# Shifting where float32r operands start in SBUF, by 64 and 128 bytes

## The chip, the cores and the metric

One core of one Trainium2 chip. The metric is the device time of one execution in microseconds: the median of the timed runs.

## What is computed

A block of two layers on a sequence of 512 tokens with 1024 channels, all in float32. Each layer has a mixer and a SwiGLU feed-forward network (FFN, inner width 2816), both between RMS norms with scales, shifts and gates that come from a condition vector:

```python
for layer in range(DEPTH):
    mod = (cond @ ada_w[layer] + ada_b[layer])[:, None, :]
    sh1, sc1, g1, sh2, sc2, g2 = jnp.split(mod, 6, axis=-1)
    u = rms_norm(h, norm_g[layer, 0]) * (1.0 + sc1) + sh1
    ...
    h = h + (1.0 + g1) * rms_norm(y, norm_g[layer, 1])
    u = rms_norm(h, norm_g[layer, 2]) * (1.0 + sc2) + sh2
    y = swiglu_ffn(u, ffn_w_in[layer], ffn_w_out[layer])
    h = h + (1.0 + g2) * rms_norm(y, norm_g[layer, 3])
```

The mixer of layer 0 is a gated recurrence (HGRN, chunks of 32 tokens, 8 heads of 128). That of layer 1 is attention in three dilated groups with 8 heads each; its input projection makes queries, keys and values for each group.

## The kernel before

**Products in three.** Weights and activations are float32. Each is cut into a float32r tile "hi" and a float32r rest "lo", and a product is three matmuls into one bank: hi by hi, hi by lo, lo by hi. `three` (lines 430 to 433) issues them, and nearly all matmuls of the kernel come from it. `block` (line 435) has weights as the stationary operand and activations as the moving one; products by token (lines 1190 and 1361, `prods` in `mixer_out` and `ffn`) have it the other way round, with 512 columns of weights moving.

**The weight stream.** `Stream` (line 36) loads 1 MB pieces of weights through SyncE's queue into two places "raw", then ScalarE copies hi and VectorE subtracts lo. hi and lo have three places each (tags "hi" and "lo" in the pool "weights"), 2048 float32r per partition. Pieces for the quarter products ("quarters", "half") are cut by the stage that uses them; it takes places of the same tags through `part_tiles` (line 119).

**Quarter products.** Part of the FFN's input product and two of the attention's value projections are done as a 2 x 2 block product with seven products in place of eight. `seven_products` (line 764) does one column block of gate and up per step. Stationary: quarters of the weights and of their sums, in the tiles hiq and loq (and, for one of two sets, the tiles "spare"). Moving: uh and ul, 256 columns at a time, or th and tl, which hold sums of quarters of the activations. Each step has seven runs of four times three matmuls, 84 in all; three runs read uh and ul, four read th and tl. There are 16 steps in layer 0's FFN and 18 in layer 1's. `seven_values` (line 1365) does the same for the values by token: here the quarters of the weights are the moving operand and uh and ul (as th and tl), apart and the like are stationary.

**Other products.** The HGRN projections, queries and keys, one value group, the mixers' output projections and the FFN's output product have 512 moving columns. After each mixer, in `mixer_out`, the first FFN blocks are done in halves of 256 columns (`half`, line 677, and lines 707 and 710). Scores, transposes and probabilities by values use plain float32.

**Where tiles lie.** Tile pools take SBUF from the left or the right side, each tile behind the last one of its pool. The pool "base" stands first on the left, with h, ident, ones, small columns, lb, omlb, uh and ul; "weights" follows with raw, hi and lo. apart lies on the right in the attention. A few tiles named "pad" only take room. In the built program before, every float32r operand of a matmul starts at 192 modulo 256 bytes in its partition, but for th and tl, which start at 128. Modulo 512 the numbers are the same.

**Order.** Most stages have their order written out by hand (`manual_schedule`); the others are ordered when the program is built.

Of the kernel before, what the change touches and what calls it, by code (L numbers as in the profile page):

```python
# [9 lines left out]
F32 = mybir.dt.float32  # L10
F32R = mybir.dt.float32r
# [4 lines left out]
P = 128  # L16
S = 512
D = 1024
KT = D // P
# [11 lines left out]
C3 = float(np.float32(TWO_PI - C1 - C2))  # L31
MAGIC = 12582912.0
WHOLE = ("quarters", "half")


class Stream:
# [41 lines left out]
    def process_to(self, end):  # L78
        while self.done < end:
            self.fill()  # L80
            i = self.done
            kind = self.items[i][0]
            t = self.raw.pop(i)
            if kind == "w":
                hi = self.pool.tile([P, 2048], F32R, name=f"hi{i}", tag="hi", bufs=self.parts)
                lo = self.pool.tile([P, 2048], F32R, name=f"lo{i}", tag="lo", bufs=self.parts)
                self.nc.scalar.copy(hi, t)  # L87
                self.nc.vector.tensor_sub(lo, t, hi.bitcast(F32))  # L88
                self.ready.append((hi, lo))
            else:  # L90
                self.items[i][2](t)
            self.done += 1
        self.fill()

    def pieces(self, n, flat=False):

        i = self.done
        t = self.raw.pop(i)
        hi = self.pool.tile([P, 2048], F32R, name=f"hi{i}", tag="hi", bufs=self.parts)
        lo = self.pool.tile([P, 2048], F32R, name=f"lo{i}", tag="lo", bufs=self.parts)  # L100
        self.ready.append((hi, lo))
        self.done += 1
        rows = 1 if flat else KT
        size = 2048 // rows // n
        cut = lambda a, k: a.rearrange("p (k c) -> p k c", k=rows)[:, :, k * size:(k + 1) * size]

        def pair(k):
            return (lambda: self.nc.scalar.copy(cut(hi, k), cut(t, k)),  # L108
                    lambda: self.nc.vector.tensor_sub(cut(lo, k), cut(t, k), cut(hi, k).bitcast(F32)))
        return [pair(k) for k in range(n)]  # L110

    def whole(self):

        assert self.items[self.done][0] in WHOLE
        self.fill()
        self.done += 1
        return self.raw.pop(self.done - 1)

    def part_tiles(self):

        self.count = getattr(self, "count", 0) + 1
        return [self.pool.tile([P, 2048], F32R, name=f"{tag}q{self.count}", tag=tag, bufs=self.parts) for tag in ("hi", "lo")]

    def take(self, ahead=None):
        ahead = self.parts - 1 if ahead is None else ahead
        k = min(self.taken + ahead, len(self.wpos) - 1)
        stop = next((i for i in range(self.done, len(self.items)) if self.items[i][0] in WHOLE), len(self.items))
        self.process_to(min(self.wpos[k] + 1, stop))
# [26 lines left out]
def block_kernel(tc, x, c, positions, ada_w, ada_b, norm_g, hgrn_w_in, lower, hgrn_norm_g, hgrn_w_out,  # L155
# [6 lines left out]
    R4 = lambda a: a.rearrange("p (r l) -> p l r", r=4)  # L162

    with ExitStack() as ctx:
        base = ctx.enter_context(tc.tile_pool(name="base", bufs=1))
        wp = ctx.enter_context(tc.tile_pool(name="weights", bufs=1))
        psum = ctx.enter_context(tc.tile_pool(name="psum", bufs=1, space=bass.MemoryType.PSUM))
# [7 lines left out]
        def fresh(p, shape, tag, bufs=1, dt=F32):  # L175
            uid[0] += 1
            return p.tile(shape, dt, name=f"{tag}{uid[0]}", tag=tag, bufs=bufs)


        tcx = ctx.enter_context(ExitStack())  # L180
        cond_tiles = tcx.enter_context(tc.tile_pool(name="tiled", bufs=1, side="right")).tile([P, KT, 32], F32, name="cond_tiles")
        pre = ctx.enter_context(ExitStack())
        sp = pre.enter_context(tc.tile_pool(name="start", bufs=1, side="right"))
        rowsC = sp.tile([8, P], F32, name="rowsC")
# [4 lines left out]

        ident = base.tile([P, P], F32, name="ident")  # L190
        make_identity(nc, ident)
        ones = base.tile([P, P], F32, name="ones")
        pool.memset(ones, 1.0)
        expo = base.tile([P, 4], F32, name="expo")
        pool.memset(expo, -0.5)
# [219 lines left out]
        st = Stream(nc, wp, items, 2, 3)  # L415
# [2 lines left out]

        lb = base.tile([P, 8], F32, name="lb")
        omlb = base.tile([P, 8], F32, name="omlb")
        uh = base.tile([P, KT, S], F32R, name="uh")
        ul = base.tile([P, KT, S], F32R, name="ul")

# [9 lines left out]
        def block(whi, wlo, c0, width, ps=None, tok=slice(0, S), kts=range(KT), u=(uh, ul)):  # L435

            ps = bank("mm") if ps is None else ps
            for kt in kts:
                a = kt * width + c0
                three(ps[:, tok], whi[:, a:a + P], wlo[:, a:a + P], u[0][:, kt, tok], u[1][:, kt, tok], kt == 0, kt == KT - 1)  # L440
            return ps
# [304 lines left out]
        def token_sums(th, tl, room, uh=uh, ul=ul):  # L746


            q = lambda a, k: a[:, k // 2 * 4:k // 2 * 4 + 4, k % 2 * 256:k % 2 * 256 + 256].bitcast(F32)
            t = [room[:, 2 * k:2 * k + 2].rearrange("p a (b n) -> p (a b) n", b=2) for k in range(4)]  # L750
            for k in (0, 1, 3, 2):
                dve.tensor_add(t[k], q(uh, k), q(ul, k))
            dve.tensor_sub(t[0], t[0], t[1])
            dve.tensor_sub(t[1], t[3], t[1])
            dve.scalar_tensor_tensor(t[3], t[0], -1.0, t[3], op0=OP.mult, op1=OP.subtract)
            dve.scalar_tensor_tensor(t[2], t[3], -1.0, t[2], op0=OP.mult, op1=OP.subtract)

            def cut():
                for k in (3, 0, 2, 1):
                    act.copy(th[:, k], t[k])  # L760
                    dve.tensor_sub(tl[:, k], t[k], th[:, k].bitcast(F32))
            return cut

        def seven_products(fs, mid, sgp, spare, th, tl):
# [12 lines left out]
            ring = []  # L777
            raw, g_of = {}, {}

            def places(i):  # L780

                p = i % 2
                if len(ring) <= p:
                    ring.append((spare if p == 0 else st.part_tiles(), st.part_tiles()))
                return ring[p]

            def r_hi(i):
                if i < len(fs):
                    raw[i] = st.whole()
                    act.copy(places(i)[0][0][:, 0:1536], raw[i][:, 512:])  # L790

            def r_lo(i):
                hi, lo = places(i)[0]
                dve.tensor_sub(lo[:, 0:1536], raw[i][:, 512:], hi[:, 0:1536].bitcast(F32))  # L794
# [13 lines left out]
            def s_cut(i, k):  # L808
                src = Q4(raw[i])[:, 1:3] if k == 0 else Q4(raw[i])[:, 0:4:3]
                return [Q4(t)[:, 2 * k:2 * k + 2] for t in places(i)[1]] + [src]  # L810
# [84 lines left out]
        def ffn(l, first, close, nxt, side):  # L895
            turns.close()
            close()
            with ExitStack() as fx:
# [4 lines left out]
                with ExitStack() as qx:  # L903
                    sgp = qx.enter_context(tc.tile_pool(name=f"sg{l}", bufs=1, side=side))
                    qp = qx.enter_context(tc.tile_pool(name=f"quarters{l}", bufs=1, side=bass.opposite_side(side)))
                    spare = [qp.tile([P, 3 * 512], F32R, name=f"spare{l}{k}") for k in range(2)]
                    qp.tile([P, 112], F32, name=f"pad_q{l}")
                    th = qp.tile([P, 4, 4, 256], F32R, name=f"th{l}")
                    tl = qp.tile([P, 4, 4, 256], F32R, name=f"tl{l}")
                    for j in range(PLAIN[l]):  # L910
                        if j == 0:
                            pss = first
                        else:
                            pss = []
                            for i in range(2):
                                w = st.take()
                                pss += [block(*w, k * P, 256) for k in range(2)]
                        sg = [fresh(sgp, [P, S], "sg", 2) for _ in range(2)]
                        for k in range(2):
                            act.activation(sg[k], pss[k], AF.Silu)  # L920
                        if j == 0:
                            cut = token_sums(th, tl, midt[:, NF - 8:])
                        for k in range(2):
                            dve.tensor_mul(mid(2 * j + k), pss[2 + k], sg[k])
                        if j == 0:
                            cut()
                            fixed.close()
                    seven_products(range(2 * PLAIN[l], NF), mid, sgp, spare, th, tl)
# [136 lines left out]
        first, vraw, vhi, vlo = {}, {}, {}, {}  # L1065
# [44 lines left out]
        tiled = lambda t: h[:, t].rearrange("p (a b) -> p a b", a=KT)  # L1110
# [103 lines left out]
        with tc.manual_schedule(engines=ORDERED):  # L1214
# [57 lines left out]
            tiles = list(vbanks)  # L1272
# [71 lines left out]
        qp = cx.enter_context(tc.tile_pool(name="h_q", bufs=1))  # L1344
# [20 lines left out]
        def seven_values(dsts, apart, th, tl):  # L1365
# [6 lines left out]
            raws, tiles = {}, {}  # L1372
# [5 lines left out]
                dve.tensor_sub(G(lo, o), src, G(hi, o).bitcast(F32))  # L1378

            def place(i, tile):  # L1380
                tiles[i, tile] = st.part_tiles()

            def prepare(i, step):
                if i >= len(dsts):
# [185 lines left out]
        for p in range(4):  # L1570
            tiles = []
# [32 lines left out]
        first = mixer_out(oT, otp, (8,), gates.pop((0, 2)), 0, "left", lambda: None)  # L1604
# [8 lines left out]
        def open_attention():  # L1613
# [20 lines left out]
            return v_prod  # L1634

        ffn(0, first, h0.close, ((1, 0), open_attention), "right")
        v_away = dpool.tile([P, NT, 512], F32, name="v_away")

# [229 lines left out]
        first = mixer_out(oT, store[0], (3, 5), gates.pop((1, 2)), 1, "left", cx.close, tail)  # L1868
# [32 lines left out]
```

## Time and profile before

| | us |
|---|---|
| median of 3 runs | 1520.79 |
| lowest, highest | 1519.11, 1520.88 |
| the profiled execution | 1520.42 |
| its span, first to last instruction | 1518.7 |
| granted TensorE clock, mean | 0.997 |

The profile is of one execution. Its timeline has a row for each matmul with the start in us from the span's beginning. The second number of a row is the time from a matmul's start to its end; matmuls overlap in the pipeline, so what a matmul costs in a stream is the distance from its start to the next one's. Rows by stage give busy time of each engine inside a stretch of the span.

### The profile page before, as it was taken

The numbers are of one execution on the slowest core, as the hardware profiler recorded it, in microseconds if no ns is written. First come the engines' busy times: TensorE is split into PE (matmuls) and PEld (weight loads), VectorE is DVE, ScalarE is ACT, GpSimd is POOL, SyncE is SP. The second block draws the span as 40 slices with busy tenths as digits, with TensorE's granted clock in tenths as the row PEclk, the third lists the DMA queues.
The fourth block names the chain that finished last, engine by engine and source line by source line (L and its number), as shares of the span: only waits on it lengthen the run. The fifth ranks groups of instructions, "written<-read, shape, count | busy, mean of one in ns | idle before, by whom it ended". The sixth has DMA issues, their size and how long they took to land. (4 is left out here: it accounts for less than half of the span.)

```text
span 1518.7 us, 23536 instructions
## 1 busy us (share of the span) xinstructions
PE 1501.0 (99%) x9231; PEld 1316.2 (87%) x9231; DVE 1061.3 (70%) x1837; ACT 719.0 (47%) x1215; POOL 235.2 (15%) x208
## 2 busy tenths in 40 slices
PE   8999999999999999999999999999999999999998
PEld 6777888898999988888987888988888899999886
DVE  4577767486888897476667766686466978888633
ACT  4433443363454433375545666356655544454231
POOL 1012211031222211140001110011002212221100
PEclk9999999999999999999999999999999999999999
DMA  9554444125333356423166540365213333334521
GB/s 308 171 175 132 160 139 167 56 84 166 112 106 104 106 196 227 152 103 125 57 194 169 149 129 29 116 190 140 83 53 116 102 94 111 112 105 147 199 106 56
DMA packets 206943, 199.14 MB, mean 131 GB/s; under 512 B 6840, under 2 KB 164720, under 8 KB 206576
## 3 DMA queue, kind: packets, MB, share of 16 engines
q1 hardware_dynamic: 203856, 190.87, 40.7%
q10 hardware_dynamic: 1952, 6.65, 1.2%
q8 instruction: 72, 1.18, 0.3%
q0 software_dynamic: 1024, 0.13, 0.2%
q14 instruction: 39, 0.32, 0.1%
HBM read 192.31 MB, written 5.31 MB: 130 GB/s over the span
## 5 line engine op out<-in xcount | busy, mean ns | idle before, releaser
L88 DVE TENSOR_TENSOR lo<-raw,hi 128x2048 fp32r<-128x2048 f32 x68 | 158.8, 2336 | 94.3 <-ACT hi L87 94.1
L87 ACT CAST hi<-raw 128x2048 fp32r<-128x2048 f32 x68 | 129.8, 1908 | 193.6 <-DMA raw<-in_ffn_w_out_dram 55.6
L431 PE MATMUL ps_mm<-apart,hi 128*128 128x512 f32 x384 | 151.4, 394 | 0.0
L432 PE MATMUL ps_mm<-apart,hi 128*128 128x512 f32 x384 | 151.2, 394 | 0.0
L433 PE MATMUL ps_mm<-apart,lo 128*128 128x512 f32 x384 | 150.7, 394 | 0.0
L431 PE MATMUL ps_mm<-uh,hi 128*128 128x512 f32 (+1 forms) x400 | 146.3, 366 | 0.0
L432 PE MATMUL ps_mm<-ul,hi 128*128 128x512 f32 (+1 forms) x400 | 144.3, 361 | 1.0 <-DVE ul L531 1.0
L433 PE MATMUL ps_mm<-uh,lo 128*128 128x512 f32 (+1 forms) x400 | 144.5, 361 | 0.0
L814 ACT CAST hiq<-raw 128x1024 fp32r<-128x1024 f32 x68 | 68.4, 1051 | 66.1 <-DVE raw L802 65.1
L431 PE MATMUL ps_mm<-hi,oh 128*128 128x512 f32 x240 | 94.0, 392 | 0.0
L432 PE MATMUL ps_mm<-lo,oh 128*128 128x512 f32 x240 | 93.4, 389 | 0.0
L431 PEld LDWEIGHTS ps_mm<-uh,hi 128*128 128x128 f32 x400 | 75.5, 189 | 19.7 <-issue 8.4
L432 PEld LDWEIGHTS ps_mm<-ul,hi 128*128 128x128 f32 x400 | 75.6, 189 | 12.1 <-DVE ul L531 1.4
L433 PEld LDWEIGHTS ps_mm<-uh,lo 128*128 128x128 f32 x400 | 75.5, 189 | 11.5
L433 PEld LDWEIGHTS ps_mm<-apart,lo 128*128 128x128 f32 x384 | 72.2, 188 | 14.9 <-DVE lo L88 0.3
L432 PEld LDWEIGHTS ps_mm<-apart,hi 128*128 128x128 f32 x384 | 72.2, 188 | 14.2
L431 PEld LDWEIGHTS ps_mm<-apart,hi 128*128 128x128 f32 x384 | 72.2, 188 | 14.0
L250 DVE SCALAR_TENSOR_TENSOR shared<-raw,cond,shared 128x512 f32<-128x512 f32 x98 | 73.3, 748 | 10.6 <-DMA raw<-in_ada_w_dram 9.7
L818 DVE TENSOR_TENSOR loq<-raw,hiq 128x1024 fp32r<-128x1024 f32 x68 | 80.0, 1218 | 0.4 <-ACT hiq L814 0.4
L252 POOL PARTITION_ALL_REDUCE shared<-shared x14 | 45.9, 3280 | 203.5 <-DVE shared L250 203.5
L798 POOL TENSOR_TENSOR raw<-raw 128x512 f32<-128x512 f32 x34 | 54.6, 1607 | 104.5 <-DVE loq L794 47.3
L802 DVE TENSOR_TENSOR raw<-raw 128x1024 f32<-128x1024 f32 x34 | 41.7, 1226 | 39.1 <-POOL raw L798 39.1
(448 smaller groups left out, 4393.9 us busy)
## 6 DMA issues: line engine op xcount, KB each, us to landing
raw<-in_ada_w_dram SPq DMA_DIRECT2D x40, 1024.0 KB, 5.2
raw<-in_ffn_w_in_dram SPq DMA_DIRECT2D x136, 256.0 KB, 3.6
raw<-in_attn_w_in_dram SPq DMA_DIRECT2D x48, 512.0 KB, 5.3
raw<-in_ffn_w_out_dram SPq DMA_DIRECT2D x22, 1024.0 KB, 4.9
raw<-in_hgrn_w_in_dram SPq DMA_DIRECT2D x12, 1024.0 KB, 5.5
raw<-in_attn_w_in_dram SPq DMA_DIRECT2D x12, 1024.0 KB, 5.2
raw<-in_ffn_w_in_dram SPq DMA_DIRECT2D x10, 1024.0 KB, 5.1
first<-in_ada_w_dram SPq DMA_DIRECT2D x14, 512.0 KB, 7.4
```

The source lines that it names most:

```text
L87: self.nc.scalar.copy(hi, t)
L88: self.nc.vector.tensor_sub(lo, t, hi.bitcast(F32))
L250: dve.scalar_tensor_tensor(a, r[:, k], sc, a, op0=OP.mult, op1=OP.add)
L252: pool.partition_all_reduce(a, a, P, bass.bass_isa.ReduceOp.add)
L431: pe.matmul(ps, ah, bh, start=start, stop=False)
L432: pe.matmul(ps, ah, bl, start=False, stop=False)
L433: pe.matmul(ps, al, bh, start=False, stop=stop)
L798: pool.tensor_add(r[:, 2], r[:, 2], r[:, 0])
L802: dve.tensor_tensor(r[:, 0:2], r[:, 0:3:2], r[:, 1:2].broadcast_to((P, 2, 512)), op=OP.add)
L814: act.copy(hi, src)
L818: dve.tensor_sub(lo, src, hi.bitcast(F32))
```

## The change

Only places in SBUF change. ones, lb and omlb leave the pool "base" for one that lives through the first part of the kernel, which moves uh, ul, raw, hi, lo and what follows on the left; a tile of 64 bytes moves the right side. The hi and lo places become 256 bytes longer, and users may start at an offset in them: R0 (16 floats, 64 bytes) in `seven_products`, V0 (32 floats, 128 bytes) in `seven_values`. Pads are fitted.

In the built program the starts modulo 256 bytes, as (moving, stationary), are:

| matmuls | count | before | after |
|---|---|---|---|
| 512 columns | 3840 | (192, 192) | (128, 128) |
| 256, halves behind the mixers | 384 | (192, 192) | (128, 128) |
| 256, FFN quarters, uh or ul moving | 1224 | (192, 192) | (128, 192) |
| 256, FFN quarters, th or tl moving | 1632 | (128, 192) | (128, 192) |
| 256, values | 672 | (192, 192) | (0, 128) |

As the hi and lo places are now 8448 bytes apart instead of 8192, their starts modulo 512 alternate between 128 and 384. Plain float32 tiles shift along, most by 64 bytes.

```diff
@@ -31,6 +31,8 @@
+R0, V0 = 16, 32
@@ -82,8 +84,7 @@
             if kind == "w":
-                hi = self.pool.tile([P, 2048], F32R, name=f"hi{i}", tag="hi", bufs=self.parts)
-                lo = self.pool.tile([P, 2048], F32R, name=f"lo{i}", tag="lo", bufs=self.parts)
+                hi, lo = self.places(i)
...
@@ -116,10 +116,14 @@
-    def part_tiles(self):
-
+    def places(self, i, first=0):
+
+        return [self.pool.tile([P, 2048 + 64], F32R, name=f"{tag}{i}", tag=tag, bufs=self.parts)[:, first:first + 2048]
+                for tag in ("hi", "lo")]
+
+    def part_tiles(self, first):
         self.count = getattr(self, "count", 0) + 1
-        return [self.pool.tile([P, 2048], F32R, name=f"{tag}q{self.count}", tag=tag, bufs=self.parts) for tag in ("hi", "lo")]
+        return self.places(f"q{self.count}", first)
@@ -162,6 +166,7 @@
+        ctx.enter_context(tc.tile_pool(name="shift", bufs=1, side="right")).tile([P, 16], F32, name="shift_r")
@@ -178,7 +183,12 @@
-        cond_tiles = tcx.enter_context(tc.tile_pool(name="tiled", bufs=1, side="right")).tile([P, KT, 32], F32, name="cond_tiles")
+        tp = tcx.enter_context(tc.tile_pool(name="tiled", bufs=1, side="right"))
+        cond_tiles = tp.tile([P, KT, 32], F32, name="cond_tiles")
+        ones = tp.tile([P, P], F32, name="ones")
+        lb = tp.tile([P, 8], F32, name="lb")
+        omlb = tp.tile([P, 8], F32, name="omlb")
+        tp.tile([P, 112], F32, name="pad_t")
@@ -189,7 +199,6 @@
-        ones = base.tile([P, P], F32, name="ones")
@@ -418,8 +427,6 @@
-        lb = base.tile([P, 8], F32, name="lb")
-        omlb = base.tile([P, 8], F32, name="omlb")
@@ -781,7 +788,7 @@
-                    ring.append((spare if p == 0 else st.part_tiles(), st.part_tiles()))
+                    ring.append((spare if p == 0 else st.part_tiles(R0), st.part_tiles(R0)))
@@ -903,8 +910,8 @@
-                    spare = [qp.tile([P, 3 * 512], F32R, name=f"spare{l}{k}") for k in range(2)]
-                    qp.tile([P, 112], F32, name=f"pad_q{l}")
+                    spare = [qp.tile([P, 3 * 512 + R0 - k * R0], F32R, name=f"spare{l}{k}")[:, R0 - k * R0:] for k in range(2)]
+                    qp.tile([P, 48], F32, name=f"pad_q{l}")
@@ -1378,7 +1385,7 @@
-                tiles[i, tile] = st.part_tiles()
+                tiles[i, tile] = st.part_tiles(V0)
```

More of the change, by code (lines that the diff above doesn't have):

```diff
@@ L98, in pieces @@
         t = self.raw.pop(i)
-        hi = self.pool.tile([P, 2048], F32R, name=f"hi{i}", tag="hi", bufs=self.parts)
-        lo = self.pool.tile([P, 2048], F32R, name=f"lo{i}", tag="lo", bufs=self.parts)
+        hi, lo = self.places(i)
         self.ready.append((hi, lo))
```

## The prediction

> **What bounds the kernel now.** I read the page first (shares of engines, clock), then the busy times by stage, then the timeline of PE alone, to see how far the starts of neighbouring matmuls lie apart.
>
> ```profile
> span 1518.7 us, 23536 instructions
> PE 1501.0 (99%) x9231; PEld 1316.2 (87%) x9231; DVE 1061.3 (70%) x1837; ACT 719.0 (47%) x1215; POOL 235.2 (15%) x208
> ...
> PEclk9999999999999999999999999999999999999999
> ```
>
> PE is busy 1501.0 of 1518.7 us at full granted clock. So the time is the matmul stream itself, and a change that moves no work can only act through the distance between starts. The busy times by stage say the same, stage by stage (columns: us, then PE, PEld, DVE, ACT, POOL busy, with counts):
>
> ```profile
> 70.00:256.00 186.00, 186.00 (x1116) 147.34 (x1114) 140.84 (x264) 71.17 (x138) 33.55 (x25) 1.00 0.49 159
> ...
> 376.00:532.00 156.00, 156.00 (x1315) 154.79 (x1314) 129.96 (x140) 74.84 (x92) 36.11 (x31) 1.00 0.37 105
> 532.00:699.00 167.00, 167.00 (x785) 139.54 (x784) 122.69 (x198) 76.21 (x115) 32.23 (x27) 1.00 0.50 165
> ...
> 1209.50:1385.00 175.50, 175.50 (x1482) 174.25 (x1481) 143.73 (x156) 81.14 (x102) 39.85 (x34) 1.00 0.37 106
> ```
>
> PE has no hole in the HGRN projections (70 to 256), in the two stages of quarter products (376 to 532, 1209.5 to 1385) or in the first FFN's second half (532 to 699). DVE is the next engine, at 83% in the quarter products.
>
> Now the distances. All float32r operands start at 192 modulo 256 bytes, except th and tl, which start at 128. First the 512-wide matmuls, and the 256-wide ones with uh and ul moving that follow them, both operands at 192:
>
> ```profile
> 310.36 0.39 PE L431 MATMUL ps_a<-hi,oh 128*128 128x512 f32 x1
> ...
> 313.08 0.28 PE L431 MATMUL ps_mm<-uh,hi 128*128 128x256 f32 x1
> 313.19 0.28 PE L432 MATMUL ps_mm<-ul,hi 128*128 128x256 f32 x1
> ...
> 313.79 0.28 PE L431 MATMUL ps_mm<-uh,hi 128*128 128x256 f32 x1
> ```
>
> From 310.36 to 313.08 lie twelve 512-wide starts: 2.72 / 12 = 226.7 ns each. From 313.19 to 313.79 lie five 256-wide ones: 120.0 ns each. The difference, 106.7 ns for 256 columns, is the streaming; what is left of either is the same **fixed 13.3 ns per matmul**, whatever the width. Then the quarter products, uh moving first, th moving after:
>
> ```profile
> 422.03 0.28 PE L431 MATMUL ps_mm<-uh,spare 128*128 128x256 f32 x1
> ...
> 423.47 0.29 PE L431 MATMUL ps_mm<-th,spare 128*128 128x256 f32 x1
> ...
> 433.23 0.29 PE L431 MATMUL ps_b<-th,hiq 128*128 128x256 f32 x1
> ```
>
> ```profile
> 446.15 0.28 PE L431 MATMUL ps_mm<-th,hiq 128*128 128x256 f32 x1
> ...
> 448.87 0.28 PE L431 MATMUL ps_mm<-th,hiq 128*128 128x256 f32 x1
> ```
>
> Twelve starts with uh moving take 1.44 us: 120.0 ns. Twenty-four with th moving (446.15 to 448.87) take 2.72 us: 113.3 ns. Lines, shape, stationary tile and waits are the same; what differs is that uh starts at 192 and th at 128. The fixed part is 6.7 ns there, **one step of 6.7 ns** lower. The whole prediction hangs on this one pair of rows.
>
> **The change part by part.** No instruction is added on PE, ACT, POOL or SP, and their order is the old one; DVE gets one more wait in the second FFN, on its own earlier work. So no DMA issues earlier or later by itself. What changes is where operands start. I write (moving, stationary) in bytes modulo 256. The layouts of both programs hold 7752 float32r matmuls: 3840 of 512 columns and 3912 of 256.
>
> 1. *Quarter products of the FFN*, 34 blocks of 84. 48 of each 84 have th or tl moving and stay at (128, 192); the 36 with uh or ul moving go from (192, 192) to the same (128, 192). This step is priced by a row of its own. A block now takes 433.23 - 423.47 = 9.76 us (both rows are the first th start after a uh run, one block apart). At 113.3 ns throughout it is 84 x 0.1133 = 9.52 us. 34 x 0.24 = **8.2 us** less. DVE is busy 143.73 us over the second stage's 18 blocks, 8.0 us a block, and stays under 9.52; if that cover were gone, its 8.0 us would be the floor, not more than now. POOL and ACT have half of their time free.
>
> 2. *512-wide matmuls*, 3840 of them, from (192, 192) to (128, 128). No row of before has (128, 128). Bounds: the fixed part can't fall below zero, 13.3 ns or two steps a matmul, 51 us in all. Upwards nothing excludes a loss; steps of 6.7 ns are what the rows show, and one step up gives 233.3 ns and 25.6 us more. I take one step down. The fixed part is the same at both widths, so it belongs to a matmul's beginning, and the one row in which the moving operand begins at 128 has it one step lower. The weights of a 512-wide matmul have twice the time to load, so where they start should count less here than in the quarter products. 3840 x 6.7 ns = **25.6 us** less; this is the big term and the weak one.
>
> 3. *256-wide halves behind the mixers* (lines 431 to 433 called by `half`, and lines 707 to 710), 384 of them, also to (128, 128). Same argument, same bounds: 384 x 6.7 ns = 2.6 us less, between 5.1 less and 2.6 more.
>
> 4. *Values*, 672 of them: the weights' quarters are the moving side here, and go from 192 to 0; uh, apart, th and tl are stationary and go from 192 to 128.
>
> ```profile
> 735.03 0.28 PE L432 MATMUL ps_a<-loq,uh 128*128 128x256 f32 x1
> ...
> 737.31 0.28 PE L433 MATMUL ps_a<-hiq,ul 128*128 128x256 f32 x1
> ```
>
> 19 starts in 2.28 us are 120.0 ns, the fixed 13.3 ns again. (0, 128) is in no row. One step less is 672 x 6.7 ns = 4.5 us; two steps would be 9.0, none 0, one up 4.5 more. I take one step, from the nearest row.
>
> 5. *float32 matmuls* (scores, flips, P times V) and the tiles that merely shift along by 64 bytes. I cost them at nothing: such matmuls' mean times do not follow the tiles they read.
>
> ```profile
> L1743 PE MATMUL ps_a<-qk,qk 128*128 128x128 f32 x128 | 17.0, 275 | 0.2 <-DVE h L1799 0.2
> ...
> L1819 PE MATMUL ps_b<-h,V 128*128 128x128 f32 x64 | 12.6, 278 | 1.5 <-ACT h L1797 1.5
> ...
> L1536 PE MATMUL ps_b<-v_tok,aT 128*128 128x128 f32 x64 | 11.0, 274 | 0.0
> ```
>
> qk starts at 64, h at 128, v_tok at 192: 275, 278 and 274 ns. Even 2 ns on each of the 1479 PE records that are not float32r (9231 less 7752) would be 3 us either way.
>
> The sum: 8.2 + 25.6 + 2.6 + 4.5 = 40.9 us less. The profiled execution took 1520.4 us (span 1518.7), 0.4 under the median of the three timed runs, 1520.8. 1520.4 - 40.9 = **1479.5 us**. Once PE is 2.7% faster nothing else is late: at 140.84 of 186 us DVE has 24% free where it is fullest among the 512-wide stages, and the DMA engines are busy half of the time.
>
> Two rules of the Trainium skill bear on this. "SBUF — State Buffer", section "Who interferes with whom", gives TensorE two independent read ports, one for the moving operand and one for the weights, and its specifications know lines of 16 bytes; by it 0, 64, 128 and 192 are all alike and the sum would be zero. The pair 120.0 and 113.3 ns above speaks against it: something on the way does see the start. "TensorE: Matmul & The Clock Gate", section "Wait — 56ns, not 53.3ns?", gives a fixed part of about 2.5 ns. By that figure an estimate of what is left to win is 10.8 ns at each 512-wide matmul, 41 us, instead of 25.6; the 6.7 ns of the th rows is the least that this trace shows.
>
> **The rivals.**
>
> *Only the distance of the two starts counts.* Both at 192: 13.3 ns. Moving 64 below stationary: 6.7. The rows read as well this way, since in them th differs from uh in its start and in its distance. Then the 512-wide matmuls and the halves, at equal starts before and after, keep 226.7 and 120 ns; the FFN gives 8.2 and the values, now 128 apart, 4.5 to 9.0. 1520.4 - 12.7 = 1507.7 us, 1503 with two steps in the values. Against it: if two streams that run side by side got in each other's way, a 512-wide matmul, which leaves its weights twice the time, should show less of it, and it shows the same 13.3 ns.
>
> *The fixed part goes almost wholly* at (128, 128), two steps for some or all of the 512-wide: up to another 25.6 + 2.6 us, 1451 to 1470 us. For it: nothing in the trace says that 6.7 is a floor. Against: no row is below it.
>
> *Nothing happens* outside the noise: 1520.4 us. It needs the th rows to be fast for another reason than their start (th and tl are also other tiles, in other places). This is what the skill's two ports would give.
>
> *Slower: equal starts at 128 cost one step more than at 192.* The place is every 512-wide matmul and the halves. 233.3 ns instead of 226.7 is 4224 x 6.7 = 28.2 us more, less 12.7 from FFN and values: 1535.9 us. It decides from 12.7 / 4224 = 3.0 ns of loss a matmul on. For it: (128, 128) is unseen, and the longer places put every second hi and lo tile 256 bytes off modulo 512, a distance that occurs nowhere in before, where all were at 192 modulo 512. Against: the one row with a moving start at 128 is the faster one.
>
> **How the numbers follow.** Chances: the forecast (1470 to 1490) 0.45, distance only (1503 to 1513) 0.20, almost wholly gone 0.10, nothing 0.05, slower 0.20. The slower case is left out, and with it the deepest end of the deep case; all others, no change among them, lie between 1455 and 1522 for 8 in 10. The forecast's own range, taken with the other faster cases, is 1455 to 1513. A measurement of this kernel tells 0.2%, 3 us, from no change. Faster by more: 0.45 + 0.20 + 0.10 = 0.75; within it 0.05; slower 0.20.
>
> **What would show each step.** In the profile of the changed kernel: (1) twelve uh starts of the quarter products 1.36 us long, and 9.52 us from block to block; (2) twelve 512-wide starts in 2.64 us, where 2.72 is the distance rival, 2.80 the slower one and under 2.60 the deep one; (3) halves and (4) values 113 ns apart; (5) PE still at 99%, and no new wait ahead of it. The prediction is wrong if the 512-wide distance does not fall, whatever the quarter products do: they hold 8 of the 41 us.

## The result and the profile after

| | before | after |
|---|---|---|
| median of 12 runs each, us | 1519.15 (1517.38 to 1522.37) | 1523.27 (1521.62 to 1527.38) |
| ratio after / before, 95% interval | | 1.0025 (1.0016 to 1.0034) |
| the profiled execution, us | 1520.42 | 1521.62 |
| its span, us | 1518.7 | 1519.9 |

The changed kernel is slower by a quarter of a per cent, about 4 us; 41 us less had been forecast. The profiled execution of after happens to be the fastest of its twelve, that of before lies above its median, so the two spans differ by only 1.2 us. The stages must be compared one by one.

The page of the changed kernel first: its span, the busy time of each engine, and the granted clock in tenths over 40 slices.

```profile
span 1519.9 us, 23537 instructions
...
PE 1501.9 (99%) x9231; PEld 1317.6 (87%) x9231; DVE 1063.5 (70%) x1837; ACT 718.2 (47%) x1215; POOL 233.9 (15%) x208
...
PEclk9999999999999999999999999999999999999999
```

PE is the bound as before: the granted clock is 1.000 after and 0.997 before, and the waits of PE add up to 11 us in both. So what PE has lost lies in the distance between its starts. The timeline of PE, at the place where before showed its 512-wide matmuls (now at (128, 128)) and the halves behind them:

```profile
308.73 0.39 PE L438 MATMUL ps_a<-hi,oh 128*128 128x512 f32 x1
...
311.45 0.28 PE L438 MATMUL ps_mm<-uh,hi 128*128 128x256 f32 x1
...
314.00 0.28 PE L438 MATMUL ps_mm<-uh,hi 128*128 128x256 f32 x1
...
315.92 0.28 PE L439 MATMUL ps_mm<-ul,hi 128*128 128x256 f32 x1
```

Twelve 512-wide starts take 311.45 - 308.73 = 2.72 us: 226.7 ns each, to the digit what they took at (192, 192). Sixteen of the halves take 1.92 us: 120.0 ns, the same too. The two terms that were to bring 28 us have brought nothing. Then a block of quarter products, where every matmul is now at (128, 192):

```profile
419.52 0.28 PE L438 MATMUL ps_b<-uh,hiq 128*128 128x256 f32 x1
...
422.34 0.28 PE L438 MATMUL ps_mm<-th,spare 128*128 128x256 f32 x1
...
423.76 0.28 PE L438 MATMUL ps_mm<-uh,spare 128*128 128x256 f32 x1
...
432.24 0.28 PE L438 MATMUL ps_b<-th,hiq 128*128 128x256 f32 x1
```

24 starts with uh moving take 422.34 - 419.52 = 2.82 us, 117.5 ns each, and 12 with th moving take 1.42 us, 118 ns. uh and th are now alike, as the same pair of starts should be. But the common value is **117.8 ns** (a block of 84 starts takes 432.24 - 422.34 = 9.90 us, and layer 0's 1344 starts take 158.29 us, 117.78 ns each), not the 113.33 ns that th had in before. For uh, at 120.0 before, that is 2.22 ns less, for th 4.45 ns more: 48 x 4.45 - 36 x 2.22 = 0.134 us more a block, 34 x 0.134 = 4.5 us. The th matmuls have the same starts modulo 256 in both kernels, and became slower all the same.

The stages as a whole, from the start of a stage's first matmul to that of the next stage's (for the last stage, layer 1's FFN output, to that of the last matmul), in the two profiled executions (us):

| stage | before | after |
|---|---|---|
| quarter products, layer 0 | 156.2 | 158.3 |
| quarter products, layer 1 | 175.7 | 178.1 |
| values, first set | 44.1 | 43.9 |
| queries and keys between the sets | 175.2 | 174.4 |
| values, second set | 46.2 | 45.8 |
| HGRN projections | 187.8 | 187.8 |
| FFN output products | 167.1, 119.5 | 167.0, 119.5 |

The quarter products give 4.5 us away, the values win 0.6 back. That is 3.9 us, and the ratio says 3.8 (0.0025 x 1519). The rest of the difference between the two spans lies in stages with waits. What stands ahead of the HGRN projections took 77.4 us before and 75.8 after. Queries and keys took from 174.2 to 178.8 us in the nine profiles of the whole kernel seen here, with the same code.

### The profile page after: what moved, and what is told of

Its sections match the earlier page's. It is cut to its first block, busy times and chain, and to the rows that moved or that the text cites. A ratio compares the mean times of both kernels' runs of the same rounds, so it can differ in the third digit from the quotient of the medians.

```text
span 1519.9 us, 23537 instructions
## 1 busy us (share of the span) xinstructions
PE 1501.9 (99%) x9231; PEld 1317.6 (87%) x9231; DVE 1063.5 (70%) x1837; ACT 718.2 (47%) x1215; POOL 233.9 (15%) x208
## 3 DMA queue, kind: packets, MB, share of 16 engines
q0 software_dynamic: 1024, 0.13, 0.2%
```

## The experiments

Every kernel was timed beside before's on the same chip, and each ratio below is to that; absolute times of different chips differ by up to 4 us for the same kernel.

Theory after the result (call it **way in**): only the distance of the two starts modulo 256 counts, and at a distance of 64 bytes a stream of 256-wide matmuls has two steady paces, 113.3 and 117.8 ns; what ran just ahead decides which of them it takes. Rival (**place**): the pace follows from where the operands lie, modulo some longer period such as 512 or 1024; since the hi and lo places are 8448 bytes apart now, (128, 192) is a mixture of two cases.

**All pairs of starts, by themselves.** A kernel of bare streams: operands at 16 moving starts (0 to 960 bytes) and 4 stationary ones, and for each of the 64 pairs a bare stream:

```python
for s in range(4):
    for m in range(16):
        three(m, s, 2, 512, 6, wide)          # 36 of 512 columns
        three(m, s, 4, 256, 4, after_wide)    # 48 of 256 columns
        three(3, 3, 4, 256, 2, equal)         # 24 at (192, 192)
        three(m, s, 4, 256, 3, after_equal)   # 36 at the pair again
```

> Computes nothing of the reference (the output is a copy of x): only streams of float32r matmuls in threes, as the kernel has them, with the moving operand's start in 16 places modulo 1024 and the stationary one's in 4 modulo 256. For each pair: 36 matmuls of 512 columns, 48 of 256 right behind them, 24 of 256 at equal starts (192, 192), 36 of 256 right behind those. Theory H (what a stream does depends on what ran ahead of it): 256-wide at 64 bytes' distance is 117.7 ns apart behind the 512-wide ones and 113.3 behind the equal ones, wherever they start. Theory A (the absolute start modulo 1024 counts; th was at 128 before, uh at 640 and th at 896 after): moving 128 with stationary 192 is 113.3 in both places, moving 384, 640 and 896 are 117.7 in both. Both: equal starts 120, 512-wide 227 at equal starts. Open: 512-wide at unequal starts; if starts matter there at all, some pair is under 227.

Its timeline, with a row for each run of alike matmuls (m128b,s192b is moving at 128, stationary at 192; L56 the 512-wide ones, L59 the 256-wide ones behind them, L62 the equal ones, L65 the 256-wide ones behind those). The next row's start less the row's own is the length of the run:

```profile
692.94 8.53 PE L56 MATMUL ps<-m0b,s128b 128*128 128x512 f32 x36
701.30 5.85 PE L59 MATMUL ps<-m0b,s128b 128*128 128x256 f32 x48
...
735.00 8.34 PE L56 MATMUL ps<-m128b,s128b 128*128 128x512 f32 x36
743.17 5.91 PE L59 MATMUL ps<-m128b,s128b 128*128 128x256 f32 x48
...
756.09 8.57 PE L56 MATMUL ps<-m192b,s128b 128*128 128x512 f32 x36
764.49 5.82 PE L59 MATMUL ps<-m192b,s128b 128*128 128x256 f32 x48
770.14 3.04 PE L62 MATMUL ps<-m192b,s192b 128*128 128x256 f32 x24
773.02 4.24 PE L65 MATMUL ps<-m192b,s128b 128*128 128x256 f32 x36
777.10 8.53 PE L56 MATMUL ps<-m256b,s128b 128*128 128x512 f32 x36
...
819.11 8.34 PE L56 MATMUL ps<-m384b,s128b 128*128 128x512 f32 x36
827.28 5.91 PE L59 MATMUL ps<-m384b,s128b 128*128 128x256 f32 x48
...
1029.44 8.40 PE L56 MATMUL ps<-m0b,s192b 128*128 128x512 f32 x36
1037.68 5.60 PE L59 MATMUL ps<-m0b,s192b 128*128 128x256 f32 x48
```

Equal starts: 743.17 - 735.00 = 8.17 us for 36 of 512 columns, 226.9 ns with the entry (226.7 inside the run). Moving at 384 over 128, equal modulo 256 but not modulo 512: 8.17 us again. 128 bytes apart: 701.30 - 692.94 = 8.36, 232.2 ns. 64 apart: 764.49 - 756.09 = 8.40, 233.3 ns. The 256-wide ones at (192, 128) take 770.14 - 764.49 = 5.65 us for 48, 117.7 ns, behind the 512-wide run, and 777.10 - 773.02 = 4.08 us for 36, 113.3 ns, behind the equal one. Same matmuls, same places, two paces. The 512-wide ones have two as well at this distance: moving at 0 over 192 (64 above it, modulo 256) takes 1037.68 - 1029.44 = 8.24 us, 228.9 ns. All 64 pairs, from the seventh matmul of each run on:

| distance of the starts modulo 256 | 512 columns, ns | 256 columns, ns |
|---|---|---|
| 0 | 226.7 to 227.1 | 119.8 to 120.1 |
| 64, either way | 233.2 to 233.4, in 2 runs of 32 228.8 to 228.9 | 113.3 or 117.8 |
| 128 | 232.2 to 232.7 | 118.6 to 118.8, or 120.0 |

(The very first run, in which PE still waited for its operands, is left out of the table.) But for the two runs at 228.9 ns, the four moving starts that are alike modulo 256 (128, 384, 640 and 896, say) agree within 0.4 ns over the same stationary one at 512 columns. Of the 256-wide runs, 29 of 32 such fours agree as closely; in the other three the odd one is always moving start 0, whose pair comes first behind those of another stationary start. Together with the two paces of (192, 128) at the same places, that speaks against *place*. (The stationary starts were not varied modulo 512 here; the kernel with twelve matmuls below settles that.) 512-wide matmuls are at their best with equal starts, which before and after both have: in these streams no start had anything to win for them.

The expectation's rule for the two paces did not hold, though. It had every pair at 64 bytes at 117.7 ns behind the 512-wide run and at 113.3 behind the equal one. In the trace 10 of the 32 such runs behind the 512-wide ones were at 113.3, and 16 of the 32 behind the equal ones at 117.8, (128, 64) among them. Two paces there are; which one a way in brings is not the same for all pairs at that distance.

"SBUF — State Buffer" in the Trainium skill, section "Who interferes with whom", has two independent read ports for TensorE. These rows show that this is not the whole story: (128, 128) at 226.9 and (192, 128) at 233.3 ns differ by the moving start alone. What the starts act on in the chip, no run here shows.

**All pairs equal, and all pairs moved.** Two arrangements of the whole kernel. In the first the quarter products and the values get equal starts, (128, 128):

```diff
-R0, V0 = 16, 32
+R0, V0 = 0, 0
...
-                    qp.tile([P, 48], F32, name=f"pad_q{l}")
+                    qp.tile([P, 64], F32, name=f"pad_q{l}")
```

> The changed kernel with both offsets at 0: every float32r operand starts at 128 modulo 256, th and tl too. If the distance of the two starts modulo 256 makes the cost (equal is dear), the quarter products' matmuls stand 120 ns apart and a block of 84 takes 10.08 us instead of 9.88 after and 9.76 before: about 34 x 0.20 = 6.7 us over the changed kernel, 1530 us, and the values stay at 120. If a moving start at 128 were cheap by itself, nothing would change against the changed kernel.

In the second the quarter products get the arrangement of before, 64 bytes lower: uh over equal starts, th and tl 64 below:

```diff
-R0, V0 = 16, 32
+R0, V0 = 0, 32
```

> The changed kernel with the FFN's offset at 0 and its pad unchanged: uh and the quarters start at 128, th and tl at 64. That is before's arrangement, 64 bytes lower: uh at its stationary operand's start, th 64 below it. Theory H, or any theory of distances alone: uh 120, th 113.3 as before, a block of 84 in 9.76 us, total about 4 us under the changed kernel, 1519 us. Theory A (absolute start modulo 1024): th is elsewhere modulo 1024 than before, so 117.7, a block 9.97 us, total 1526.

Their timelines of PE, first start with th moving in two neighbouring blocks. All equal:

```profile
425.59 0.28 PE L438 MATMUL ps_mm<-th,spare 128*128 128x256 f32 x1
...
435.67 0.28 PE L438 MATMUL ps_b<-th,hiq 128*128 128x256 f32 x1
```

Moved by 64:

```profile
423.56 0.29 PE L438 MATMUL ps_mm<-th,spare 128*128 128x256 f32 x1
...
433.32 0.29 PE L438 MATMUL ps_b<-th,hiq 128*128 128x256 f32 x1
```

All equal: 10.08 us a block, 84 x 120.0 ns; the kernel took 1530.32 us (1528.19 to 1532.06), ratio 1.0069 (1.0056 to 1.0082). Moved by 64: 9.76 us a block as in before, stages 156.2 and 175.7, and 1519.24 us (1517.42 to 1520.81), ratio 0.9999 (0.9990 to 1.0008). Both came out as the theory had them. The second also undoes one part of the change: the edit takes the quarters, th and tl 64 bytes back and leaves all else as in after. uh is at equal starts again, and the loss is gone.

**The ways in.** Bare streams again: 24 512-wide matmuls at (128, 128), as ahead of the quarter products in after, then some 256-wide ones at another pair, then 96 at the pair of interest, and at the end a run of 1200 and runs behind float32 matmuls.

```python
for goal in ((2, 3), (1, 2), (0, 2)):                # (128,192), (64,128), (0,128)
    for km, ks in ((3, 3), (2, 2), (3, 2), (2, 3)):  # the pair ahead
        for count in (0, 1, 2, 3, 6, 12):
            stream(2, 2, 2, 512, 4)
            kick(km, ks, count)
            stream(*goal, 4, 256, 8)
```

> Computes nothing of the reference: matmul streams alone. Each stretch: 24 matmuls of 512 columns at (128, 128), as ahead of the changed kernel's quarter products; then 0, 1, 2, 3, 6 or 12 single 256-wide matmuls at (192, 192), (128, 128), (192, 128) or (128, 192); then 96 of 256 at a goal: (128, 192), (64, 128) or (0, 128). At the end 1200 at (128, 192) behind 12 at (192, 192), and the same goal behind 1 to 8 float32 matmuls. Theory H (two steady states, chosen by the way in): with none ahead (128, 192) runs at 117.7 ns as in the changed kernel; some kind and count of matmuls ahead brings it to 113.3, and it stays there for all 96 and all 1200; float32 matmuls may throw it out again. Rival R (113.3 is a leftover of the run ahead and wears off): the 1200 fall back to 117.7.

Its timeline (L61 the matmuls ahead, L56 the streams):

```profile
35.44 11.47 PE L56 MATMUL ps<-m128b,s192b 128*128 128x256 f32 x96
46.75 5.63 PE L56 MATMUL ps<-m128b,s128b 128*128 128x512 f32 x24
52.22 0.28 PE L61 MATMUL ps<-m192b,s192b 128*128 128x256 f32 x1
52.33 11.06 PE L56 MATMUL ps<-m128b,s192b 128*128 128x256 f32 x96
63.23 5.63 PE L56 MATMUL ps<-m128b,s128b 128*128 128x512 f32 x24
68.69 0.40 PE L61 MATMUL ps<-m192b,s192b 128*128 128x256 f32 x2
68.92 11.47 PE L56 MATMUL ps<-m128b,s192b 128*128 128x256 f32 x96
80.23 5.63 PE L56 MATMUL ps<-m128b,s128b 128*128 128x512 f32 x24
...
273.60 0.40 PE L61 MATMUL ps<-m192b,s128b 128*128 128x256 f32 x2
273.84 11.06 PE L56 MATMUL ps<-m128b,s192b 128*128 128x256 f32 x96
...
478.84 0.40 PE L61 MATMUL ps<-m192b,s192b 128*128 128x256 f32 x2
479.07 11.05 PE L56 MATMUL ps<-m64b,s128b 128*128 128x256 f32 x96
489.96 5.62 PE L56 MATMUL ps<-m128b,s128b 128*128 128x512 f32 x24
...
1271.57 136.18 PE L56 MATMUL ps<-m128b,s192b 128*128 128x256 f32 x1200
1407.59 0.38 PE L69 MATMUL ps<-h 128*128 128x128 f32 x2
```

Straight out of the 512-wide run, 96 matmuls at (128, 192) take 46.75 - 35.44 = 11.31 us: 117.8 ns, the pace of after. With one matmul at (192, 192) in between they take 63.23 - 52.33 = 10.90 us, 113.3 ns once the first few are through. With two of them it is 80.23 - 68.92 = 11.31 us, 117.8 ns again, with three, six or twelve 113.3. With two at (192, 128) it is 113.3. One at (128, 128) brings 113.3 as well, two, three, six or twelve 117.8. The pair (64, 128), at the same distance, answers otherwise: one at (192, 192) leaves it at 117.8, two bring 489.96 - 479.07 = 10.89 us, 113.3 ns once the first few are through. Twelve at (128, 128), as ahead of th in the kernel moved by 64, bring it 113.3 too. And the pace stays: 1407.59 - 1271.57 = 136.02 us for 1200, 113.4 ns. Behind one, two, four or eight float32 matmuls (two records each) the first twelve come at 124.7 ns, the rest at 117.8; only the first of these four streams follows a fast one. So the pace is a state: one matmul can set it, hundreds keep it. The distance says which paces a pair can have; which of them it takes depends on what runs ahead and on the pair, and no rule for this was found. It has to be read from a stream.

**Twelve matmuls ahead of the quarter products.** If the way in is all, twelve more 256-wide matmuls at (192, 192) ahead of each stage must turn the changed kernel's 117.8 into 113.3. Their sums go to a place of the bank that the first product overwrites:

```diff
+KICKS = 12
...
+                if i == 0:
+                    for _ in range(KICKS):
+                        pe.matmul(half(0, 0), R[0][:, 0:P], uh[:, 0, 16:272], start=True, stop=True)
                 run(half(0, 0), R, 0, B11)
```

> The changed kernel with 12 more matmuls of 256 columns at (192, 192) ahead of the first quarter product of each FFN (their sums are overwritten by the first real product). Theory H: uh and th alike then run at 113.3 ns through 1344 and 1512 matmuls, a block of 84 takes 9.52 us instead of 9.88: 34 x 0.36 = 12.4 us less, 24 x 0.12 = 2.9 us more, 1513.8 us, 9.5 under the changed kernel and about 5 under before. Rival R: the first block or two at most are faster, 1525 us.

1514.38 us (1513.25 to 1516.22), ratio 0.9963 (0.9949 to 0.9977). Its timeline of PE, the same two starts (lines of `three` are one further down):

```profile
424.26 0.28 PE L439 MATMUL ps_mm<-th,spare 128*128 128x256 f32 x1
...
433.78 0.28 PE L439 MATMUL ps_b<-th,hiq 128*128 128x256 f32 x1
```

9.52 us a block, 113.3 ns for uh and th alike: the block that the prediction had for after. All operands of the products lie where they lie in after, so *place* is ruled out in the kernel too. 24 matmuls whose sums are thrown away made the changed kernel 9 us faster (ratios 0.9963 and 1.0025).

**Two matmuls, at two pairs.** This separates the way in from the mere delay that extra matmuls bring, and from a warming-up of some kind: in the bare streams two at (192, 192) changed nothing and two at (192, 128) did. The edit is the one above with `KICKS = 2`, and for the second kernel the stationary operand `R[0][:, 48:176]`, which starts at 128.

> The changed kernel with 2 matmuls at (192, 192) ahead of each FFN's quarter products, in place of 12. In the bare streams 1, 3, 6 and 12 of these led to 113.3 ns and 2 led to 117.8. Theory H (two steady states, the way in picks one, and the stream shows which): no gain, a block of 84 stays at 9.88 us, 1523.5 us. Rival (any unequal-to-equal disturbance in front frees the stream): 9.52 us, 1511.

> The same, with the 2 matmuls at (192, 128): in the bare streams every count of these led to 113.3 ns. Theory H: both FFN stages at 9.52 us a block, 12.4 us under the changed kernel less 0.5 for the four matmuls: 1511.4 us, 8 under before. If the 12 of the earlier run worked by their number, or by the pause they make, no gain: 1523.5.

Two at (192, 192), timeline of PE:

```profile
381.50 0.40 PE L843 MATMUL ps_mm<-uh,spare 128*128 128x256 f32 x2
...
422.72 0.28 PE L439 MATMUL ps_mm<-th,spare 128*128 128x256 f32 x1
...
432.62 0.28 PE L439 MATMUL ps_b<-th,hiq 128*128 128x256 f32 x1
```

Two at (192, 128):

```profile
383.50 0.40 PE L843 MATMUL ps_mm<-uh,spare 128*128 128x256 f32 x2
...
423.19 0.28 PE L439 MATMUL ps_mm<-th,spare 128*128 128x256 f32 x1
...
432.71 0.28 PE L439 MATMUL ps_b<-th,hiq 128*128 128x256 f32 x1
```

9.90 and 9.52 us a block. Beside 1522.63 us for before on that chip: 1527.41 (1524.09 to 1529.39), ratio 1.0030 (1.0020 to 1.0040), like after; and 1514.05 (1512.43 to 1517.22), ratio 0.9945 (0.9932 to 0.9957), 8.4 us under before by the ratio. Two matmuls ahead of each of the two stages, 0.24 us long, whose sums nothing reads, decide over the pace of all that follows in it. The two kernels differ only in the 128 columns that these matmuls have as stationary operand, starting at 192 or at 128.

**Values at 64 bytes' distance.** The values are at (0, 128); at (64, 128) their stream too could have the fast pace.

```diff
-R0, V0 = 16, 32
+R0, V0 = 16, 48
```

> The changed kernel with the values' offset at 192 bytes instead of 128: moving quarters 64, stationary 128, a distance of 64 as in the FFN. Theory H: 672 matmuls at 117.7 or 113.3 ns instead of 118 to 120 on the mean, by the state in which they fall; 0 to 4.4 us less than the changed kernel, 1519 to 1523 us. If only equal or unequal counts, nothing changes.

1523.75 us (1521.06 to 1525.07), ratio 1.0023 (1.0012 to 1.0034): like after, just outside what was expected. Its timeline of PE shows the pace change in the kernel itself:

```profile
731.38 0.28 PE L438 MATMUL ps_mm<-hiq,apart 128*128 128x256 f32 x1
...
732.44 0.28 PE L438 MATMUL ps_mm<-hiq,apart 128*128 128x256 f32 x1
733.81 1.78 PE L1732 MATMUL ps_a<-qk,qk 128*128 128x128 f32 x8 [1.09 <-ACT qk L1709]
...
735.56 0.28 PE L440 MATMUL ps_mm<-hiq,apart 128*128 128x256 f32 x1
...
737.72 0.28 PE L438 MATMUL ps_mm<-hiq,apart 128*128 128x256 f32 x1
```

Nine starts in 1.06 us, 117.8 ns, ahead of a wait and eight records of float32 scores; nineteen in 2.16 us, 113.7 ns, behind them. So float32 matmuls do not always bring the slow pace, as they did in the bare streams for (128, 192). The two sets of values took 43.1 and 44.2 us, 2.4 less than in after. The total does not show it: the queries and keys between them took 176.8 us in that profile instead of 174.4. The busy times of the stretch from 772 to 951 us (columns as in the prediction), with the values at (64, 128) first:

```profile
772.00:951.00 179.00, 174.89 (x877) 146.13 (x877) 123.22 (x348) 106.19 (x222) 23.48 (x19) 1.00 0.46 133
```

and of after:

```profile
772.00:951.00 179.00, 176.90 (x898) 148.55 (x897) 125.27 (x354) 109.21 (x228) 24.04 (x20) 1.00 0.46 131
```

PE is idle for 4.1 us of it in the one and 2.1 in the other, all of it inside the queries and keys. The waits of this stage vary without the values' help: it took 178.8 us with two matmuls at (192, 192), where the values were as in after. That the waits eat such a gain regularly is not shown.

**Both together**: two matmuls at (192, 128), and the values at (64, 128).

> The same, and the values' offset at 192 bytes too (distance 64), where the earlier run showed the values' matmuls at 113 to 114 ns and the time of the whole unchanged. If that gain is eaten by waits in the query and key stages behind the values: 1511 us as without it. If the earlier run's stages were only unlucky: 3 us less, 1508.

1512.81 us (1511.00 to 1515.71), ratio 0.9943 (0.9929 to 0.9956). That is the fastest version seen, but only 1.2 us under the one with the two matmuls alone, which the spread of either covers. In the two profiled executions the queries and keys took 177.7 us with the values at (64, 128) and 177.5 without, so here the waits ate almost nothing of the 2.3 us that the values' two stages won. The values' part is still not shown in the total.

## Why the prediction was wrong, point by point

What held: PE bounds the kernel at 99% before and after, no wait took the place of the old ones, the float32 matmuls and shifted tiles cost nothing that can be seen, and a change of starts does change the distance between matmuls.

1. *Quarter products, 8.2 us less*: 4.5 us more. The counts were right; the failed step is the price, "a row of its own" with 113.3 ns for (128, 192). That row was not the price of a pair of starts but of a pair and its history. In before every stretch of th matmuls came in from uh matmuls at equal starts; in after the stream comes in from 512-wide matmuls at (128, 128), takes the pace of 117.8 ns and, having no other pair in it, keeps it to the end of the stage. That the th rows could move up at all, although the table of the change lists them as unchanged, was not considered. With the way in mended by two matmuls, the block has the forecast 9.52 us, and the two stages 152.6 and 171.6 us, 7.7 less than before.

2. *512-wide matmuls, 25.6 us less*: nothing, 226.7 ns. This term carried most of the error. The failed step: the 6.7 ns between uh and th was put down to the moving operand's beginning at 128, and carried over to (128, 128). The one pair of rows had two differences, start and distance, and the prediction said so in its rival; the argument against the rival, that a stream twice as long should show less of a clash, was no evidence. "The same 13.3 ns at both widths" comes from one value for each of two widths, at one pair of starts; streaming time and fixed part were both solved from these two, so they could not disagree. The bare streams show the opposite sign: a distance that helps 256 columns (113.3 or 117.8 for 120.0) costs 512 columns 2 to 7 ns.

3. *Halves, 2.6 us less*: nothing, 120.0 ns, for the same reason.

4. *Values, 4.5 us less*: 0.6 less. The distance is 128 there, not 64; the bare streams have 118.7 or 120.0 ns for it, at best 672 x 1.3 ns = 0.9 us.

5. *float32 and the shifts at nothing*: right within what the stages show.

Of the rivals, distance only (0.20) had the right variable and named terms 2 and 3 as nothing, but with 1507.7 us it had the same wrong price for the quarter products, and 4.5 us or more for the values, which won 0.6. The slower rival had its place and price wrong: equal starts at 128 cost what they cost at 192. That the time rose at all, for which the prediction had 0.20, bears out none of that rival's working. Nor was its distance of 256 bytes modulo 512 new: in the built program before, 48 of the 512-wide matmuls (those with the tile late as the moving operand) start at 448 over 192 modulo 512, and seven of them from 70.16 us on take 1.59 us, 227 ns each. The slower side came about by a mechanism that was not among the cases, and the range, whose upper end stood 1.6 us above no change, missed the time by 1.3 us.

## What to carry to other kernels

A distance between matmuls that is read from one row is the pace of a stream after what ran ahead of it; before it is used as a price, look for rows with the same operands behind something else. When two rows differ in two things, a bare stream over all combinations settles which one counts, before 3840 matmuls are moved. And a stream that was alike throughout kept the pace it was let in with, over up to 1512 matmuls here: at float32r with 256 columns and 64 bytes between the starts, two throw-away matmuls at another pair ahead of each of two stages brought 12 us in 1520 beside the changed kernel without them, and 8 beside before (ratios 0.9945 and 1.0025).

## What the runs showed of the hardware that was not expected

- With a new stationary operand for every float32r matmul, the distance of its two starts modulo 256 bytes set the paces that occurred. 512 columns were best at equal starts (226.7 to 227.1 against 228.8 to 233.4 ns), 256 columns at 64 bytes between them (113.3 or 117.8 against 120.0).
- At 64 bytes there were two paces, 4.4 to 4.5 ns apart at both widths (the faster one of 512 columns in 2 runs of 36 matmuls). Ahead of (128, 192), one matmul at (192, 192) lets the fast one in, two do not, three, six and twelve do; 1, 2, 3, 6 and 12 at (192, 128) all do, none at (128, 192) itself does. Ahead of (64, 128) the same list reads otherwise: one or three at (192, 192) leave the slow pace, two, six and twelve bring the fast one. The fast pace held over 1200 matmuls. Float32 matmuls in between brought the slow one to (128, 192) in the bare streams; float32 scores let the fast one in at (64, 128) in the kernel.
- At a distance of 128 bytes and 256 columns there were two as well, 118.6 to 118.8 and 120.0 ns. What in the chip keeps such a state was not tried and stays open.
